# Seven buffers and a new order for the first adaLN weights, and the second condition's adaLN products on ScalarE and GpSimd, in a two-layer diffusion backbone step

## The chip, the cores and the metric

The kernel runs on one core of a Trainium2 chip. The time is in microseconds (us) of device time for one execution; less is better. The engines are called PE (TensorE, the matrix engine), DVE (VectorE), ACT (ScalarE), POOL (GpSimd) and SP (SyncE, which issues the transfers).

## The reference

One step of a hybrid backbone of two layers over 10 tiles of 128 tokens: eight tiles of latent tokens and two of context tokens, 1024 features each. What matters here is the start of a layer:

```python
def _rmsnorm(x, g):
    xf = x.astype(F32)
    y = xf * lax.rsqrt(jnp.mean(xf * xf, axis=-1, keepdims=True) + EPS)
    return (y * g.astype(F32)).astype(x.dtype)

def _adaln(cond, w, b):
    m = jax.nn.silu(cond) @ w + b
    shift, scale, gate = jnp.split(m[:, None, :], 3, axis=-1)
    return shift, scale, gate
```

Every layer does RMSNorm, multiplies by 1 + scale and adds shift, runs its mixer, multiplies by gate and adds the residual. There are two conditions: c for the latent tokens and c_ctx for the context tokens, so the product with the adaLN weights (1024 x 3072 for each layer) is needed for two vectors. Layer 0's mixer (here AB) starts with one projection (`w_in_ab`) that feeds windowed attention and an mLSTM memory with input and forget gates. Layer 1's (C) is latent attention. The output is the new tokens and the new caches and states.

## The kernel before, in words

The whole step is one program, written with helpers that record each operation. Apart from a middle part whose order is written by hand, a scheduler sets the order of the instructions on each engine; the program gives tiles, their buffers and the order in which work is asked for. A tile belongs to a tag with a number of buffers, and a new tile of the tag waits until the oldest one is no longer read.

*The start* (`layer_ab`, L718). A string of letters sets the order in which two sorts of work are asked for. For `x`, one token tile is loaded (`load_x`, L675, tag `xin`, 512 KB), normalised by its root mean square, and later transposed by PE (`xT_tile`, L522) and modulated (`xT_mod`, L533: on DVE, with a copy by ACT at L538 and a subtraction by DVE or POOL at L539 that splits the value into a high and a low half, `hTh` and `hTl`). For `m`, one of eight column groups of layer 0's shift and scale is made: `mod_load` (L239) loads two weight tiles of 128 columns each (tag `wm`, 512 KB each), `mod_start` (L252) multiplies them with both conditions on PE (`S<-wm,condT`), copies the result into a row (`mrow`, L262), and `columns` turns the row to columns by two small transposes (`S<-small,mrow`). The list `late` holds work back by two letters. At the letter of index 12 the weights of the first dense block are asked for (`blocks[0].load()`).

*The dense phase.* Then PE multiplies all tokens with `w_in_ab`, in blocks of 256 columns (the first has 272). Each block's weights are loaded (`wf`), ACT copies the high half (`wh`, L354) and POOL subtracts to get the low half (`wl`, L355). PE makes three products for each pair, high by high, high by low and low by high (L103 in the profile, the helper of all matmuls; transposes are at L107). The features come in eight parts, so a result takes 24 matmuls: 272 columns wide for each of ten token tiles in the first block, 512, 512 and 256 tokens wide in the others. A convolution (`cx`, L1465 on POOL, L1468 to L1475 on DVE) follows some blocks.

*The gates.* Woven into the dense phase is `gates` (L1294): it transposes the gate values (`GI`, `GF`), runs scans over tokens on DVE (L1371 to L1378), makes `LI` (L1401) and `rst` (L1410) and transposes both on PE again.

*The other adaLN columns* (`mod_steps`, L286) aren't made on PE: in each of eight steps a weight tile `mw` (128 x 512) is loaded, and DVE multiplies it by one number for each partition and adds it to `macc`, once for each condition (`cd` 0 and 1; L319 for the first step, L321 for the other seven). At the end PE sums `macc` over the partitions (`S<-macc,unit`) and DVE adds the bias (`bmod`, L306). Six blocks of 512 columns are made beside the dense phase, and blocks of 256 columns later, for layer 1's gate, in layer C.

Of the kernel before, what the change touches and what calls it, by code (L numbers as in the profile page):

```python
# [10 lines left out]
F32 = mybir.dt.float32  # L11
# [3 lines left out]
ALU = mybir.AluOpType  # L15
# [4 lines left out]
D = 1024  # L20
# [5 lines left out]
KD = D // 128  # L26
# [117 lines left out]
def body(tc, I, O, dbg=None, stop_at=None):  # L144
    K = Kern(tc, I, O, dbg)
    with ExitStack() as ctx:
        K.const = ctx.enter_context(tc.tile_pool(name="const", bufs=1))
        K.dram = ctx.enter_context(tc.tile_pool(name="dram", bufs=1, space=DRAM))
        K.left = lambda n: tc.alloc_tile_pool(name=n, bufs=1, side="left", reuse_waits="tile")
        K.right = lambda n: tc.alloc_tile_pool(name=n, bufs=1, side="right", reuse_waits="tile")  # L150
        K.set_psum(S=6, T=2)
        setup_consts(K)
        layer_ab(K)
        layer_c(K)
        K.set_psum()
# [84 lines left out]
def mod_load(K, pool, k):  # L240

    ws = []
    for i in range(2):
        w = K.t(pool, [128, KD, 128], F32, "wm", 4)
        f = slice(i * D + k * 128, i * D + (k + 1) * 128)
        K.dma(w, K.I["w_mod"][0, :, f].rearrange("(k p) f -> p k f", p=128))
        ws.append(w)
    return ws
# [37 lines left out]
def mod_steps(K, p, blocks, ahead, width=512):  # L286


    nc = K.nc
    parts = [(l, f, k) for l, f in blocks for k in range(KD)]  # L290
    asked = []

    def ask():
        if parts:
            l, f, k = parts.pop(0)
            w = K.t(p, [128, width], F32, "mw", ahead)
            K.dma(w, K.I["w_mod"][l, k * 128:(k + 1) * 128, f:f + width])
            asked.append(w)

    def total(l, f, acc):  # L300
        ps = K.ps()
        for cd in range(2):
            K.mm(ps[0:2, 0:width], K.sel[cd], acc[:, cd], cd == 0, cd == 1)
        bm = K.t(p, [2, width], F32, "bmod", 1)
        K.dma(bm, K.I["b_mod"][l:l + 1, f:f + width].to_broadcast([2, width]))
        nc.vector.scalar_tensor_tensor(bm, ps[0:2, 0:width], 0.5, bm, ALU.mult, ALU.add)  # L306
        K.dma(K.modd[l][:, f:f + width], bm)

    for _ in range(ahead):
        ask()  # L310
    late = None
    for l, f in blocks:
        acc = K.t(p, [128, 2, width], F32, "macc", 2)
        for k in range(KD):
            w = asked.pop(0)
            for cd in range(2):
                c = K.condT[:, cd * KD + k:cd * KD + k + 1]
                if k == 0:
                    nc.vector.tensor_scalar(acc[:, cd], w, c, None, ALU.mult)  # L319
                else:  # L320
                    nc.vector.scalar_tensor_tensor(acc[:, cd], w, c, acc[:, cd], ALU.mult, ALU.add)  # L321
            ask()
            if late and k == 5:
                late()
                late = None
            yield
        late = partial(total, l, f, acc)
    if late:
        late()
# [164 lines left out]
def rstd_of(K, pool, ss, n, eps, tag):  # L494
    nc = K.nc
    w = ss.shape[1]
    r = K.t(pool, [128, w], F32, tag, 4)
    nc.vector.tensor_scalar(r, ss, 1.0 / n, eps, ALU.mult, ALU.add)
    nc.gpsimd.tensor_tensor(r, r, K.mhalf.to_broadcast([128, w]), ALU.pow)
    return r  # L500
# [51 lines left out]
def x_src(K, tt):  # L552
    if tt < 8:
        return K.I["x_sample"][0, tt * 128:(tt + 1) * 128, :]
    return K.I["x_prompt"][0, (tt - 8) * 128:(tt - 7) * 128, :]
# [94 lines left out]
def layer_ab(K):  # L650
    nc, I = K.nc, K.I
# [20 lines left out]
    sp = left("start")  # L672
    setup_cond(K, sp)

    def load_x(tt):  # L675
        x = K.t(sp, [128, D], F32, "xin", 6)
        K.dma(x, x_src(K, tt))
        ss = K.t(sp, [128, 1], F32, "xss", 4)
        jk = K.t(sp, [128, D], BF16, "xjk", 1)
        nc.scalar.activation(jk, x, AF.Square, accum_out=ss)  # L680
        r = rstd_of(K, sp, ss, D, EPS, "xr")
        nc.vector.tensor_scalar(x, x, r[:, 0:1], None, ALU.mult)
        return x
# [4 lines left out]
    dense = Dense(blocks)  # L688
# [3 lines left out]
    def start_x(tt):  # L692
        x = load_x(tt)
        ci, i = chunk_of(tt)

        def rest():
            xT_tile(K, x, xT[ci][:, :, i * 128:(i + 1) * 128])
            if i == CHUNKS[ci][1] // 128 - 1:
                ready.append(ci)
                for j in done:  # L700
                    xT_mod(K, 0, ci, j, xT[ci][:, j, :])

        return rest

    def start_mod(k):
        ws = mod_load(K, sp, k)
        fin = mod_start(K, sp, k, ws)

        def rest():
            fin()  # L710
            done.append(k)
            for ci in ready:
                xT_mod(K, 0, ci, k, xT[ci][:, k, :])

        return rest

    xs, ks = iter(range(NT)), iter(range(KD))
    for n, a in enumerate("mxmxmxmxmxmxmxmxxx"):  # L718
        late.append(start_x(next(xs)) if a == "x" else start_mod(next(ks)))
        if n == 12:  # L720
            blocks[0].load()
        if len(late) > 2:
            late.pop(0)()
# [12 lines left out]
    zs[3].parts = 4  # L736
    mp = left("mod")
    dense.mods = mod_steps(K, mp, mods[0:2], 4)
    K.tp = gtp = left("gtmp")
    dense.run(1, 1)  # L740
# [4 lines left out]
    mp.release()  # L745
    mp = left("mod1")
    dense.mods = mod_steps(K, mp, mods[2:], 4)
    dense.run(3, 0.9)
    for _ in dense.mods:
        pass  # L750
    mod_cols(K, 1, mp)
# [5 lines left out]
    w = I["w_out_ab"][0]  # L757
# [40 lines left out]
    p = left("wo2")  # L798
# [11 lines left out]
    sp = right("cst")  # L810
# [1102 lines left out]
def layer_c(K):  # L1913
# [23 lines left out]
    nc.vector.tensor_scalar(ncol[:, 0:3], ps[:, 0:3], QSC, None, ALU.mult)  # L1937
    nc.vector.tensor_copy(ncol[:, 3:5], ps[:, 3:5])
    dense.mods = mod_steps(K, cm, [(1, 2 * D + f) for f in range(0, D, 256)], 4, 256)
    dense.run(3, 0.8)  # L1940
    for _ in dense.mods:
# [412 lines left out]
```

## Time and profile before

| What | Value |
|---|---|
| Three runs | 2618.43, 2617.19, 2615.36 us, median 2617.19 |
| Profiled execution | 2614.64 us, its span 2612.8 us |
| PE busy | 2563.6 us (98%) |
| DVE busy | 1779.5 us (68%) |
| ACT busy | 1411.7 us (54%) |
| POOL busy | 1161.8 us (44%) |

The span runs from the first to the last instruction of the profiled execution. A line of the table by stretch gives the busy time of each engine in a stretch of the span, with the number of instructions, PE's granted clock (1.00 is full speed), the share of the 16 DMA engines, and GB/s. A line of the waits names who waits, on which line, for whom, and us in total, times, and the longest. A line of groups gives the operation, its tiles (out<-in), shape and count, then busy us and mean ns of one, and the idle time before them. A line of the timeline gives the start, the duration, the operation, and in brackets the idle time before it and what ended it.

### The profile page before, as it was taken

What the parts mean: (1) busy time and instruction counts of PE and PEld (TensorE: products, weight loads), DVE (VectorE), ACT (ScalarE), POOL (GpSimd) and SP (SyncE); (2) the same over time, 40 slices, a digit from 0 to 9 for tenths busy, and PEclk for the clock granted to TensorE, in tenths of its full rate; (3) what the DMA queues carried; (4) which work ended last, traced back from release to release, by engine and by line L of the source; (5) the groups of instructions that cost most, each with busy time, mean ns of one, the idle gap of its engine ahead of it and who ended that gap; (6) DMA issues with size and microseconds to landing.
All of it is one profiled execution on the core that took longest, in us unless ns stands there. A gap on an engine that the chain in (4) does not pass through costs nothing. (4 is left out here: it accounts for less than half of the span.)

```text
span 2612.8 us, 48325 instructions
## 1 busy us (share of the span) xinstructions
PE 2563.6 (98%) x16233; PEld 2259.4 (86%) x16233; DVE 1779.5 (68%) x4045; ACT 1411.7 (54%) x3608; POOL 1161.8 (44%) x1549
## 2 busy tenths in 40 slices
PE   7999999999999999999999999999999999999998
PEld 6888898898898888887888878898899989999887
DVE  6994565656647676477777546526788888888754
ACT  5232444444434433477666433234788888888842
POOL 4342333423324344356445453224455545555832
PEclk9999999999999999999999999999999999999999
DMA  7565576566667664445443453523310101101333
GB/s 249 155 183 174 163 208 189 160 197 188 179 199 212 204 211 153 135 150 161 120 126 106 130 193 133 160 73 101 88 36 27 45 27 38 36 28 29 120 99 131
DMA packets 352970, 347.23 MB, mean 133 GB/s; under 512 B 36073, under 2 KB 297878, under 8 KB 352466
## 3 DMA queue, kind: packets, MB, share of 16 engines
q1 hardware_dynamic: 352722, 344.14, 43.2%
q8 instruction: 129, 2.11, 0.3%
q14 instruction: 119, 0.97, 0.1%
HBM read 233.52 MB, written 110.51 MB: 132 GB/s over the span
## 5 line engine op out<-in xcount | busy, mean ns | idle before, releaser
L355 POOL TENSOR_TENSOR wl<-wf,wh 128x256 fp32r<-128x256 f32 (+3 forms) x288 | 241.7, 864 | 435.8 <-ACT wh L354 381.2
L103 PE MATMUL mm<-hTh,wh 128*128 128x512 f32 (+1 forms) x912 | 329.0, 361 | 0.9 <-DVE scr L621 0.9
L103 PE MATMUL mm<-hTh,wl 128*128 128x512 f32 (+1 forms) x912 | 325.1, 356 | 0.0
L103 PE MATMUL mm<-hTl,wh 128*128 128x512 f32 (+1 forms) x912 | 325.0, 356 | 0.0
L103 PE MATMUL S<-cK,cQ 96*128 96x512 f32 (+3 forms) x1248 | 296.9, 364 | 2.2 <-ACT cPa L2256 1.3
L2304 DVE TENSOR_TENSOR cpl<-T,cph 128x512 fp32r<-128x512 f32 x336 | 228.6, 686 | 45.9 <-ACT cph L2303 42.8
L103 PEld LDWEIGHTS S<-cK,cQ 96*128 96x128 f32 (+1 forms) x1248 | 193.3, 189 | 25.4 <-ACT cPa L2256 3.5
L2303 ACT CAST cph<-T 128x512 fp32r<-128x512 f32 x336 | 192.4, 591 | 29.8 <-PE T L107 18.6
L103 PEld LDWEIGHTS mm<-hTh,wl 128*128 128x128 f32 x912 | 171.7, 188 | 26.6
L103 PEld LDWEIGHTS mm<-hTh,wh 128*128 128x128 f32 x912 | 171.6, 188 | 24.9 <-DVE scr L621 1.1
L103 PEld LDWEIGHTS mm<-hTl,wh 128*128 128x128 f32 x912 | 171.7, 188 | 23.2
L2254 DVE TENSOR_REDUCE cmx<-S 128x1 f32<-128x512 f32 x256 | 173.2, 682 | 16.7 <-PE S L103 15.2
L103 PE MATMUL V<-cph,cV 128*128 128x256 f32 x672 | 177.2, 290 | 1.1 <-DVE co L2319 0.8
L103 PE MATMUL V<-cpl,cV 128*128 128x256 f32 x672 | 172.1, 284 | 0.3 <-DVE cpl L2304 0.3
L1174 ACT CAST att_ph<-mm 128x512 fp32r<-128x512 f32 x168 | 98.6, 587 | 102.0 <-PE mm L107 100.7
L2235 POOL TENSOR_SCALAR cPa<-cPa,cst 128x512 f32<-128x512 f32 x128 | 98.7, 771 | 118.2 <-DVE cst L2232 97.6
L354 ACT CAST wh<-wf 128x256 fp32r<-128x256 f32 (+3 forms) x288 | 101.8, 409 | 74.9 <-DMA wf<-in_w_in_ab 42.8
L103 PE MATMUL mm<-wh,hTh 128*128 128x256 f32 x480 | 136.9, 285 | 4.0 <-DVE scr L1488 4.0
L1175 DVE TENSOR_TENSOR att_pl<-mm,att_ph 128x512 fp32r<-128x512 f32 x168 | 115.8, 689 | 34.8 <-ACT att_ph L1174 29.2
L1163 POOL TENSOR_SCALAR att_p<-att_p,att_den 128x640 f32<-128x640 f32 (+1 forms) x128 | 97.4, 774 | 86.9 <-DVE att_den L1160 39.1
L103 PE MATMUL mm<-wl,hTh 128*128 128x256 f32 x480 | 135.3, 282 | 0.1
L103 PE MATMUL mm<-wh,hTl 128*128 128x256 f32 x480 | 135.3, 282 | 0.0
(456 smaller groups left out, 7887.6 us busy)
## 6 DMA issues: line engine op xcount, KB each, us to landing
wf<-in_w_in_ab SPq DMA_DIRECT2D x120, 256.0 KB
in<-in SPq DMA_DIRECT2D x40, 514.0 KB
in<-in SPq DMA_DIRECT2D x32, 386.0 KB
mw<-in_w_mod SPq DMA_DIRECT2D x48, 256.0 KB
in<-scr SPq DMA_DIRECT2D x40, 258.0 KB
o_x<-y SPq DMA_DIRECT2D x20, 512.0 KB
wm<-in_w_mod SPq DMA_DIRECT2D x16, 512.0 KB
in<-cx SPq DMA_DIRECT2D x32, 256.0 KB
```

The costliest lines, as they stand in the source:

```text
L103: return self.nc.tensor.matmul(out, lhsT, rhs, start=start, stop=stop)
L354: K.nc.scalar.copy(wh, wf[:, k])
L355: K.nc.gpsimd.tensor_sub(wl, wf[:, k], wh.bitcast(F32))
L1163: nc.gpsimd.tensor_scalar(pv, pv, den[:, i:i + 1], 1.0, ALU.mult, ALU.mult)
L1174: K.nc.scalar.copy(ph, self.T)
L1175: K.nc.vector.tensor_sub(pl, self.T, ph.bitcast(F32))
L2235: nc.gpsimd.tensor_scalar(pv, pv, wt[:, c:c + 1], rd, ALU.mult, ALU.mult)
L2254: nc.vector.tensor_reduce(mx[:, b, c:c + 1], S, AX.X, ALU.max, negate=True)
L2303: nc.scalar.copy(ph, T_)
L2304: nc.vector.tensor_sub(pl, T_, ph.bitcast(F32))
```

## The change

The tag `wm` has seven buffers instead of four, `xin` four instead of six. The string of the start keeps eight `m` and ten `x` but has four pairs, then four `m`, then six `x`. In `mod_steps`, for blocks of 512 columns and the second condition (`cd` 1), the seven steps after the first are made by ACT, which multiplies the weight tile into a new tile `mq` (two buffers), and POOL, which adds it to `macc`: 42 operations of DVE become 42 of ACT and 42 of POOL. Lines from `mod_steps` on have numbers higher by four.

```diff
@@ mod_load
-        w = K.t(pool, [128, KD, 128], F32, "wm", 4)
+        w = K.t(pool, [128, KD, 128], F32, "wm", 7)
@@ mod_steps
                 if k == 0:
                     nc.vector.tensor_scalar(acc[:, cd], w, c, None, ALU.mult)
+                elif cd == 0 or width < 512:
+                    nc.vector.scalar_tensor_tensor(acc[:, cd], w, c, acc[:, cd], ALU.mult, ALU.add)
                 else:
-                    nc.vector.scalar_tensor_tensor(acc[:, cd], w, c, acc[:, cd], ALU.mult, ALU.add)
+                    q = K.t(p, [128, width], F32, "mq", 2)
+                    nc.scalar.mul(q, w, c)
+                    nc.gpsimd.tensor_add(acc[:, cd], acc[:, cd], q)
@@ layer_ab
-        x = K.t(sp, [128, D], F32, "xin", 6)
+        x = K.t(sp, [128, D], F32, "xin", 4)
...
-    for n, a in enumerate("mxmxmxmxmxmxmxmxxx"):
+    for n, a in enumerate("mxmxmxmxmmmmxxxxxx"):
```

SP's queue at the start, where the transfers of token tiles (`xin`), adaLN weights (`wm`) and the first dense weights (`wf`) are issued, before:

```order
L138 DMA xin_232<-in_x_sample 128x1024
L138 DMA xin_281<-in_x_sample 128x1024
L138 DMA xin_330<-in_x_sample 128x1024
L138 DMA xin_379<-in_x_sample 128x1024
L138 DMA xin_443<-in_x_sample 128x1024
L138 DMA wf_487<-in_w_in_ab 128x2x256
L138 DMA wf_487<-in_w_in_ab 128x2x16
L138 DMA wf_490<-in_w_in_ab 128x2x256
L138 DMA wm_253<-in_w_mod 128x8x128
L138 DMA wf_490<-in_w_in_ab 128x2x16
L138 DMA wm_255<-in_w_mod 128x8x128
L138 DMA wm_302<-in_w_mod 128x8x128
```

The same rows after the change:

```order
L138 DMA xin_232<-in_x_sample 128x1024
L138 DMA wm_253<-in_w_mod 128x8x128
L138 DMA wm_255<-in_w_mod 128x8x128
L138 DMA xin_281<-in_x_sample 128x1024
L138 DMA wm_302<-in_w_mod 128x8x128
L138 DMA xin_330<-in_x_sample 128x1024
L138 DMA wf_497<-in_w_in_ab 128x2x256
L138 DMA wf_497<-in_w_in_ab 128x2x16
L138 DMA wm_304<-in_w_mod 128x8x128
L138 DMA wf_500<-in_w_in_ab 128x2x256
L138 DMA wf_500<-in_w_in_ab 128x2x16
L138 DMA wm_351<-in_w_mod 128x8x128
```

The weight tiles wm_253 to wm_351 have moved ahead of the third and later token tiles, which are now issued between or behind them.

PE around the first matmul of the dense phase (`S_778<-wh`), before; `T` are transposes of token tiles, `S<-wm` products with adaLN weights:

```order
L107 MATMUL T_686<-small,xin_629 128x128 x4
L107 MATMUL T_692<-small,xin_629 128x128 x4
L103 MATMUL S_416<-wm_414,condT 2x128 x8
L107 MATMUL S_435<-small,mrow_372 128x2 x2
L103 MATMUL S_468<-wm_464,condT 2x128 x8
L103 MATMUL S_468<-wm_466,condT 2x128 x8
L107 MATMUL S_531<-small,mrow_433 128x2 x2
L103 MATMUL S_564<-wm_560,condT 2x128 x8
L103 MATMUL S_564<-wm_562,condT 2x128 x8
L107 MATMUL S_583<-small,mrow_485 128x2 x2
L107 MATMUL S_621<-small,mrow_581 128x2 x2
L103 MATMUL S_778<-wh_493,hTh_129 128x272
```

After the change:

```order
L103 MATMUL S_461<-wm_457,condT 2x128 x8
L107 MATMUL S_480<-small,mrow_400 128x2 x2
L107 MATMUL S_541<-small,mrow_447 128x2 x2
L107 MATMUL T_617<-small,xin_566 128x128 x4
L107 MATMUL T_623<-small,xin_566 128x128 x4
L103 MATMUL S_461<-wm_459,condT 2x128 x8
L107 MATMUL T_638<-small,xin_587 128x128 x4
L107 MATMUL T_644<-small,xin_587 128x128 x4
L107 MATMUL S_558<-small,mrow_478 128x2 x2
L103 MATMUL S_778<-wh_503,hTh_129 128x272
L103 MATMUL S_778<-wl_504,hTh_129 128x272
L103 MATMUL S_778<-wh_503,hTl_130 128x272
```

The transposes of the last two token tiles, which stood ahead of the dense phase, have moved into it, and one row of columns (mrow_478) stands right ahead of it where two stood.

POOL behind the start, before, where `wl` are the low halves of dense weights:

```order
L1368 MEMSET gB 36x1280
L1369 MEMSET gM 36x1280
L355 TENSOR_TENSOR wl_763<-wf_750,wh_762 128x256
L355 TENSOR_TENSOR wl_767<-wf_750,wh_766 128x256
L355 TENSOR_TENSOR wl_771<-wf_760,wh_770 128x256
L355 TENSOR_TENSOR wl_775<-wf_760,wh_774 128x256
L355 TENSOR_TENSOR wl_1203<-wf_1198,wh_1202 128x256
L355 TENSOR_TENSOR wl_1207<-wf_1198,wh_1206 128x256
L355 TENSOR_TENSOR wl_1213<-wf_1200,wh_1212 128x256
L355 TENSOR_TENSOR wl_1217<-wf_1200,wh_1216 128x256
```

After the change, with the additions to `macc` at L325:

```order
L1372 MEMSET gB 36x1280
L1373 MEMSET gM 36x1280
L325 TENSOR_TENSOR macc_906<-macc_906,mq_942 128x512
L325 TENSOR_TENSOR macc_906<-macc_906,mq_978 128x512
L325 TENSOR_TENSOR macc_906<-macc_906,mq_1014 128x512
L325 TENSOR_TENSOR macc_906<-macc_906,mq_1050 128x512
L325 TENSOR_TENSOR macc_906<-macc_906,mq_1095 128x512
L359 TENSOR_TENSOR wl_763<-wf_750,wh_762 128x256
L325 TENSOR_TENSOR macc_906<-macc_906,mq_1140 128x512
L359 TENSOR_TENSOR wl_767<-wf_750,wh_766 128x256
L359 TENSOR_TENSOR wl_771<-wf_760,wh_770 128x256
L359 TENSOR_TENSOR wl_775<-wf_760,wh_774 128x256
```

Six additions of the second condition now stand in this queue ahead of and between the low halves, which keep their order.

DVE at the gates, between the first scan (`gM`) and the next ones (`gB`), before; `cx` is the convolution:

```order
L1468 SCALAR_TENSOR_TENSOR cx_1567<-scr_1524,cw,cx_1567 128x512
L306 SCALAR_TENSOR_TENSOR bmod_1532<-S_1529,bmod_1532 2x512
L1378 SCALAR_TENSOR_TENSOR gM<-LF,m_1363,LI 4x1024 x2
L1371 SCALAR_TENSOR_TENSOR gB<-rst,LF 4x1280
L1372 SCALAR_TENSOR_TENSOR gB<-rst,LF 4x1280
L1378 SCALAR_TENSOR_TENSOR gM<-LF,LI 4x256 x2
```

After the change:

```order
L1479 SCALAR_TENSOR_TENSOR cx_1593<-scr_1597,cx_1593 128x512
L1382 SCALAR_TENSOR_TENSOR gM<-LF,m_1381,LI 4x1024 x2
L1456 MEMSET scr_1639 128x1
L1462 MEMSET scr_1639 128x1
L1479 SCALAR_TENSOR_TENSOR cx_1602<-scr_1606,cx_1602 128x512
L306 SCALAR_TENSOR_TENSOR bmod_1654<-S_1651,bmod_1654 2x512
L1472 SCALAR_TENSOR_TENSOR cx_1643<-scr_1639,cw,cx_1643 128x256
L1375 SCALAR_TENSOR_TENSOR gB<-rst,LF 4x1280
L1376 SCALAR_TENSOR_TENSOR gB<-rst,LF 4x1280
L1382 SCALAR_TENSOR_TENSOR gM<-LF,LI 4x256 x2
```

The scans keep their order, but two convolution steps and the bias (`bmod`) now stand between the first scan and the next ones, where nothing stood.

More of the change, by code (lines that the diff above doesn't have):

```diff
@@ L747, in layer_ab @@
     dense.mods = mod_steps(K, mp, mods[2:], 4)
-    dense.run(3, 0.9)
+    dense.run(3,0.9)
     for _ in dense.mods:
```

## The prediction

> **What bounds the kernel now.** I read the page first (its line of busy times), then the busy time by stretch of the program, then the waits of TensorE (PE).
>
> ```profile
> PE 2563.6 (98%) x16233; PEld 2259.4 (86%) x16233; DVE 1779.5 (68%) x4045; ACT 1411.7 (54%) x3608; POOL 1161.8 (44%) x1549
> ```
>
> TensorE is busy for 2563.6 of 2612.8 us, so everything that can be won without removing matmuls lies in 49 us of idle time and in time at a low clock. The table by stretch says where. Its columns are length, busy PE, weight loads, VectorE (DVE), ScalarE (ACT), GpSimd (POOL), granted clock, DMA share, GB/s.
>
> ```profile
> 6.60:16.00 9.40, 9.37 (x65) 6.31 (x65) 1.20 (x5) 2.97 (x6) 0.73 (x2) 1.00 1.08 375
> 16.00:57.60 41.60, 34.52 (x287) 25.50 (x286) 35.15 (x66) 28.68 (x63) 25.74 (x29) 1.00 0.88 278
> 57.60:66.00 8.40, 8.38 (x55) 8.37 (x56) 7.60 (x20) 2.90 (x6) 5.77 (x6) 0.80 0.04 5
> 66.00:130.00 64.00, 64.00 (x388) 54.10 (x386) 58.39 (x120) 15.69 (x40) 22.87 (x21) 1.00 0.52 157
> 130.00:149.00 19.00, 14.96 (x89) 12.63 (x89) 17.81 (x34) 8.88 (x15) 11.99 (x8) 0.91 0.35 88
> 180.00:230.00 50.00, 50.00 (x374) 44.50 (x374) 33.67 (x60) 9.57 (x27) 11.50 (x12) 1.00 0.63 194
> 230.00:1074.00 844.00, 839.00 (x5424) 758.46 (x5423) 506.67 (x1306) 351.97 (x933) 320.15 (x398) 1.00 0.62 188
> ```
>
> Three things are to be seen. The start (16 to 57.6) leaves PE idle for 7.1 us. The stretch where the gates are computed (130 to 149) leaves 4.0. From 230 on PE is full, 839 of 844 us: what is won before that point is carried to the end, and nothing in the part behind can pay back or eat much. Note DVE in 66 to 130: 58.39 of 64, yet PE is full there, so a lighter DVE wins nothing in that stretch. The waits of PE behind the start, in us (total, times, longest), name what is left:
>
> ```profile
> PE S L107 <- ACT mrow L262: 3.2, 1, 3.2
> PE T L107 <- ACT rst L1410: 2.2, 1, 2.2
> PE T L107 <- DVE LI L1401: 1.6, 1, 1.6
> PE S L103 <- DVE bmod L306: 1.4, 1, 1.4
> ```
>
> These 8.4 us and the idle time of the start are all that the change can reach before 230.
>
> **Change, part 1: order of the start, seven weight buffers, four token buffers.** The dense phase begins when all eight adaLN columns are there. Work of PE up to that point, and the rate of the loads (the same table columns as above), and the last steps:
>
> ```profile
> L103 PE MATMUL S<-wm,condT 128*2 128x128 f32 x193 | 22.5, 273 | 0.0
> L107 PE MATMUL T<-small,xin 128*128 128x128 f32 x80 | 11.6, 282 | 3.7 <-DVE xT L528 2.7 <-ACT xT L530 0.9
> L107 PE MATMUL S<-small,mrow 2*128 2x2 f32 x14 | 2.0, 207 | 0.2 <-ACT mrow L262 0.2
> ...
> 0.00:6.00 6.00, 0.04 (x1) 0.04 (x1) 0.85 (x6) 1.59 (x2) 0.19 (x4) 1.00 0.56 162
> 6.00:42.00 36.00, 32.17 (x248) 23.26 (x249) 22.28 (x49) 23.30 (x48) 16.05 (x20) 1.00 1.07 351
> 42.00:48.00 6.00, 6.00 (x55) 4.45 (x53) 5.25 (x8) 2.94 (x8) 4.95 (x6) 1.00 0.91 278
> ```
>
> ```profile
> 46.33 0.37 SPq L138 DMA_DIRECT2D wm<-in_w_mod  x1
> 57.62 0.28 PE L107 MATMUL S<-small,mrow 2*128 2x2 f32 x2 [3.25 <-ACT mrow L262]
> 57.83 0.39 PE L103 MATMUL S<-wh,hTh 128*128 128x272 f32 x1
> ```
>
> Now all ten tokens go through before the dense phase, and the last weight tile is issued only at 46.33. In the new order tokens 8 and 9 are transposed inside the dense block.
> - By PE: 22.5 + 11.6 + 2.0 = 36.1 us of work stand between 16.0 and the dense start; two of ten tokens less are 16/80 x 11.6 = 2.3 us less. 16.0 + 33.8 gives 49.8 as the earliest start.
> - By DMA: up to the last weight tile the new order loads 16 x 0.524 MB of weights, 8 x 0.524 of tokens, 4 x 0.278 of dense weights and 0.4 of small ones, 14.1 MB. The rows move 0.97 MB by 6 us and 12.6 more by 42, at 278 GB/s the rest: all is there at 44. Behind it come the last products, the row, its columns and the modulation; from 46.33 plus a load to 57.83 these took at most 11.5 us now, so 44 lands between 50 and 53.
>
> I take 50.3: 7.5 us earlier than 57.83. The 2.3 us of transposes are not saved, they move behind the start: **A = -5.2 us** (ends: start at 47.5 gives -8, at 53.5 gives -2.0). Freed token buffers are not missed: at four, a token's load waits for the one four earlier, and the tokens now come late. On SP each load that waits for its buffer holds all behind it; the weights, which had four buffers, no longer wait.
>
> The clock:
>
> ```profile
> 60.00:61.00 1.00, 1.00 (x6) 1.00 (x6) 1.00 (x5) 0.73 (x2) 0.49 (x1) 0.50 0.00 0
> 62.00:63.00 1.00, 1.00 (x8) 1.00 (x8) 1.00 (x3) 0.59 (x2) 0.09 (x1) 0.73 0.00 0
> 146.00:148.00 2.00, 2.00 (x7) 1.61 (x7) 2.00 (x4) 0.09 (x1) 0.00 (x0) 0.53 0.07 15
> ```
>
> Shortly after the pause of 3.25 us at 57.62 the granted clock was 0.50; by the stretch 57.6 to 66 (0.80 over 8.4 us) that costs 8.4 x 0.20 = 1.7 us. It came again after the 2.2 us pause at 142.76 (0.91 over 19 us: 1.7 us). With no long wait for the last row ahead of the dense start the first one goes: **B = -1.7** (0 if a wait stays). The Trainium skill ("TensorE: Matmul & The Clock Gate", Part 1: The HAM clock gate) has a throttle that closes after a free-running window of some 3.4 us without work. The trace agrees on the length of the slow time but shows it after a pause of 2.2 us too. By the page alone B would be the same.
>
> **Part 2: the gates.** The order moves the gate work against the matmuls, so the two waits there are recomputed.
>
> ```profile
> 113.07 1.05 PE L107 MATMUL T<-small,GF 128*36 128x128 f32 x8
> ...
> 119.86 0.28 PE L103 MATMUL S<-hTl,wh 128*128 128x256 f32 x1
> 119.98 0.28 PE L103 MATMUL S<-hTh,wl 128*128 128x256 f32 x1
> ...
> 124.80 0.40 PE L103 MATMUL S<-hTl,wh 128*128 128x512 f32 x1
> 125.03 0.40 PE L103 MATMUL S<-hTh,wl 128*128 128x512 f32 x1
> ...
> 134.19 0.78 PE L107 MATMUL T<-small,LI 36*128 36x36 f32 x10 [1.61 <-DVE LI L1401]
> ```
>
> ```profile
> 132.03 2.02 DVE L1401 TENSOR_TENSOR LI<-LI,gB 36x1280 f32<-36x1280 f32 x1
> 130.68 0.71 ACT L354 CAST wh<-wf 128x256 fp32r<-128x256 f32 x2 [8.88 <-DMA wf<-in_w_in_ab]
> ```
>
> From GF's transposes to LI the chain on DVE takes 134.05 - 113.07 = 21.0 us, and PE covers 134.19 - 113.07 - 1.61 = 19.5 of it. A wide matmul costs 0.23 us (125.03 - 124.80), a half one 0.12. In the new order 48 wide and 29 half ones stand there instead of 56 and 24: 1.2 us less cover, 18.3. DVE's own order puts two convolution steps and a bias (0.5 to 0.8 us each) between the scans and takes one out behind them, some 1.3 us more, so the chain becomes 22.3 and the wait 4.0. Between LI and rst nine wide ones come to four half ones less, 1.6 us more cover, and DVE has about as much less to do there, so the 2.2 us wait goes to 0. **C = 4.0 + 0 - 1.6 - 2.2 = +0.2**; the low clock stays, since a pause of 4.0 is left. Ends: all 3.8 go and the clock with them, -5.5; or the last GF copy is late. That copy stands on ACT behind two casts that now wait for dense weights (8.88 us in the row of ACT): +4.
>
> **Part 3: 42 products from DVE to ACT and POOL.** Prices, of DVE's product, POOL's subtraction of dense weights, POOL's subtraction of the tokens, which has the new addition's shape, ACT's cast of that shape, and POOL's convolution:
>
> ```profile
> L321 DVE SCALAR_TENSOR_TENSOR macc<-mw,condT,macc 128x512 f32<-128x512 f32 x84 | 67.1, 839 | 7.3 <-DMA mw<-in_w_mod 7.2
> L355 POOL TENSOR_TENSOR wl<-wf,wh 128x256 fp32r<-128x256 f32 x40 | 44.3, 1134 | 68.4 <-ACT wh L354 57.3 <-PE S L103 11.1
> L539 POOL TENSOR_TENSOR hTl<-xT,hTh 128x512 fp32r<-128x512 f32 x8 | 11.9, 1491 | 9.0 <-ACT hTh L538 9.0
> L538 ACT CAST hTh<-xT 128x512 fp32r<-128x512 f32 x16 | 9.4, 618 | 11.6 <-DVE xT L537 11.6
> L1465 POOL TENSOR_SCALAR cx<-scr,cw 128x512 f32<-128x512 f32 x8 | 9.1, 1135 | 22.0 <-ACT scr L1450 12.3 <-PE S L103 7.6 <-DVE scr L1458 2.1
> ```
>
> ```profile
> 206.65 4.34 POOL L355 TENSOR_TENSOR wl<-wf,wh 128x256 fp32r<-128x256 f32 x4 [11.06 <-PE S L103]
> ```
>
> DVE loses 42 x 0.839 = 35.2 us, POOL gains 42 x 1.49 = 62.6, ACT 42 x 0.62 = 26.0 (priced by the cast), and all of this lies beside a full PE. What comes to the path is the order on POOL: it works its queue in order, so the weight halves (wl), for which PE waits, stand behind additions that wait for loads. Five dense blocks fill 66 to 235, 34 us each; each needs 8 x 1.13 + 3 x 1.1 = 12.4 us of POOL, and eight additions 11.9: 24.3 of 34. There is room. With less DVE work the 1.4 us wait for bmod goes: **D = -1.4** (0). Two new waits are likely. In the dense start the tiles' results are emptied from PSUM by DVE, which then still modulates tokens 8 and 9, so that a bank comes free about one or two of its 0.84 us instructions late, 1 us. And the second condition's sum, which now passes two engines, reaches its selecting matmul about one addition later, 1 us after what PE has to do meanwhile: **E = +2.0** (0 to +8). Layer C is scheduled anew as well; PE is full there: **F = 0** (-3 to +3).
>
> The Trainium skill ("SBUF — State Buffer", SBUF: two separate sides) speaks against this part: a DVE operation with two inputs in SBUF and a GpSimd one hold a shared port against each other, one waits for the whole other. In the trace four wl took 4.34 us while DVE ran products, 1.09 each, so they were hindered and not shut out. By the rule 42 additions of 1.49 would shut DVE out for 62.6 us to save it 35.2.
>
> Sum: -5.2 - 1.7 + 0.2 - 1.4 + 2.0 = **-6.1**. The profiled execution took 2614.64 us (span 2612.8 and 1.8 around it), 2.55 below the median of the runs. 2608.5 for a profiled one, 2611.1 against the median of 2617.19; I say 2611.
>
> **Rivals.**
> - *Better*: both waits at the gates and their low clock go (C = -5.5). For it: the wait of 1.6 is short, and DVE is lighter by 14 products ahead of GF. Against: the order leaves less cover. -5.2 - 1.7 - 5.5 - 1.4 + 2.0 = -11.8: 2605.4.
> - *The loads set the start*: the rate (1.07 of the DMA engines up to 42 us) is the limit, the dense phase begins at 53.5, and a wait for the last row stays. A = -2.0, B = 0: -1.2, 2616.0. That is the change not doing what it says.
> - *The gates eat it*: the last GF copy waits on ACT for dense weights; C = +4.2: -2.1, 2615.1.
> - *Slower: POOL falls behind.* Additions contended by DVE's products. From 2.7 us for one ((34 - 12.4) / 8) POOL is over its 34 us per block and PE waits for wl; with wl at the price of a contended one it is earlier. At 3.2 us each it is 4 us over per block, 5 blocks, +20: -6.1 + 20 = +13.9, 2631. For it: POOL's prices vary with DVE's work. Against: 1.49 is a price measured beside a busy DVE (7.60 of 8.40 us).
>
> **How the numbers follow.** A measurement of this kernel can tell about 0.2% from no change, 5.2 us: faster is below 2612.0, slower above 2622.4. Forecast 0.45, better 0.17, loads 0.13, gates 0.13, POOL 0.10, nothing at all 0.02. The forecast lies just inside faster, so I count 0.27 of it as faster and 0.18 as same; with the better case and 0.06 of the two middle ones faster is 0.50, same 0.40, slower 0.10. The range leaves out POOL's case and the outer part of the better one: 2603 to 2620.
>
> **What would show it.** Right: the first 272 wide matmul near 50 us, clock 1.00 behind it, a wait of about 4 us for LI, none for rst and bmod, PE's busy time from 230 on unchanged. Wrong: the dense start after 53, PE waiting for wl or for macc for more than 3 us in all, additions of over 2.5 us, or a different idle time of PE behind 1000 us.

## The result, and the profile after

The changed kernel took 2631.5 us (median of 4 runs, 2630.5 to 2633.35) against 2617.69 for the kernel before (4 runs): a ratio of 1.0053, 95% interval 1.004 to 1.0065. It is 13.8 us slower. The forecast was 2611, with a range of 2603 to 2620. Two executions among the experiments below took far longer at a low clock (4199.82 us with the new start and a light DVE, 3125.91 with the products alone and memsets), and all medians below leave them out.

The dense phase began as early as forecast, but most of what follows it did not come as forecast. Here is the table by stretch of the changed kernel, with the columns of before:

```profile
16.00:57.60 41.60, 38.98 (x330) 30.91 (x329) 30.25 (x56) 26.11 (x55) 21.72 (x25) 1.00 0.87 283
57.60:66.00 8.40, 5.51 (x42) 5.07 (x40) 8.40 (x11) 2.77 (x5) 5.96 (x5) 1.00 0.00 1
66.00:130.00 64.00, 60.37 (x348) 49.88 (x349) 60.53 (x123) 29.73 (x68) 49.82 (x41) 0.97 0.55 167
130.00:149.00 19.00, 12.91 (x68) 11.22 (x67) 18.61 (x29) 3.62 (x7) 10.28 (x6) 0.84 0.22 54
149.00:180.00 31.00, 29.41 (x192) 25.04 (x191) 27.04 (x41) 13.28 (x26) 17.74 (x16) 0.99 0.51 140
180.00:230.00 50.00, 41.85 (x295) 38.01 (x295) 40.95 (x49) 20.50 (x44) 38.55 (x30) 0.90 0.69 213
```

Up to 57.6 TensorE (PE) is busier by 4.5 us. Behind that it is idle in every stretch, 8.2 us of it in 180 to 230, where it had no idle time before, and its granted clock fell to 0.90. POOL went from 22.87 to 49.82 us in 66 to 130, and DVE did not become lighter there: 60.53 instead of 58.39. The waits of PE in the first 300 us:

```profile
PE T L107 <- DVE scr L1456: 6.1, 1, 6.1
PE S L107 <- DVE crow L217: 6.0, 1, 6.0
PE T L107 <- DVE xin L686: 4.8, 2, 2.8
PE S L103 <- ACT wh L358: 3.9, 1, 3.9
PE T L107 <- DVE GI L1334: 3.3, 1, 3.3
PE S L103 <- POOL wl L359: 2.9, 4, 1.6
PE S L103 <- POOL macc L325: 2.4, 1, 2.4
```

The 6.0 for `crow` was there before too. The first line is the wait for LI (its tile is named in the row of 144.97 below; DVE ran a small instruction at that moment). The timeline of PE at the places that count, the changed kernel:

```profile
49.98 0.39 PE L103 MATMUL S<-wh,hTh 128*128 128x272 f32 x1
...
60.70 0.40 PE L103 MATMUL S<-wh,hTh 128*128 128x272 f32 x1 [0.38 <-ACT hTh L542]
...
66.32 1.06 PE L107 MATMUL T<-small,xin 128*128 128x128 f32 x8 [2.83 <-DVE xin L686]
...
144.97 1.25 PE L107 MATMUL T<-small,LI 36*128 36x36 f32 x10 [6.09 <-DVE scr L1456]
...
208.06 0.79 PE L103 MATMUL S<-wh,hTh 128*128 128x256 f32 x2 [3.91 <-ACT wh L358]
...
245.21 0.50 PE L103 MATMUL mm<-hTh,wh 128*128 128x512 f32 x1
```

The last row is the first matmul of the hand-ordered part, which stood here before:

```profile
227.41 0.50 PE L103 MATMUL mm<-hTh,wh 128*128 128x512 f32 x1
```

It comes 17.8 us later, and the rows add up to that. The dense start is 7.85 us earlier. Two tokens' transposes inside it take 2.1, waits there 0.4 + 2.8. The waits for GI (3.3) and LI (6.1 for 1.6) add 7.8, those for wl, wh and macc 9.3 (2.7 more for wl, 3.9 for wh, 2.4 + 0.3 for macc); rst and bmod give back 3.6. That is +11.0. The low clock cost 3.4 us before (two times 1.7) and costs 1.9 + 3.0 + 0.3 + 5.0 = 10.2 now (lost share times length, from 66 on in the table): +6.8. Together 17.8. PE's last matmul came 15.9 us later, so 1.9 us came back behind 245 us. What gave them back is not shown: the same matmuls were 17.4 us late at 1087 us of the kernel before, 16.3 at 1509 and 18.1 at 1844.

### The profile page after: what moved, and what is told of

The parts are those of the page before. It is cut to its first block, busy times and chain, and to the rows that moved or that the text cites. A ratio compares the mean times of both kernels' runs of the same rounds, so it can differ in the third digit from the quotient of the medians.

```text
span 2628.7 us, 48416 instructions
## 1 busy us (share of the span) xinstructions
PE 2569.5 (98%) x16233; PEld 2263.6 (86%) x16233; DVE 1786.9 (68%) x4003; ACT 1439.5 (55%) x3650; POOL 1223.1 (47%) x1591
## 4 chain that ended last, share of the span: by engine, by line
PE 82%; DVE 3%; issue 3%; DMA 2%; ACT 2%; POOL 2%; SPq 1%; POOLq 0%; DVEq 0%; ACTq 0%
PE mm L103 33%; PE S L103 27%; PE V L103 9%; PE T L107 6%; PE D L103 3%; PE mm L107 3%; SPq L138 1%; DMA mw<-in_w_mod 1%; PE T L103 1%; POOL wl L359 1%; DMA o_x<-y 0%; DMA w<-in_w_out_ab 0%; DVE cx L1472 0%; POOL w L913 0%; DMA att_q<-ql 0%
## 5 line engine op out<-in xcount | busy, mean ns | idle before, releaser
L103 PEld LDWEIGHTS mm<-hTl,wh 128*128 128x128 f32 x912 | 171.7, 188 | 23.2
L1179 DVE TENSOR_TENSOR att_pl<-mm,att_ph 128x512 fp32r<-128x512 f32 x168 | 115.7, 689 | 35.2 <-ACT att_ph L1178 29.7
L103 PEld LDWEIGHTS V<-cph,cV 128*128 128x128 f32 x672 | 126.5, 188 | 8.3 <-DVE co L2323 1.4
```

The lines of the kernel that those rows point to most:

```text
L103: return self.nc.tensor.matmul(out, lhsT, rhs, start=start, stop=stop)
L1179: K.nc.vector.tensor_sub(pl, self.T, ph.bitcast(F32))
```

## The experiments

Each kernel was timed beside the kernel before. P is the theory that the products on ScalarE (ACT) and GpSimd (POOL) cost; P1 puts it down to POOL's queue, P2 to additions and DVE's products that hinder each other. O is the theory that the new start costs: O1 by the order of its letters, O2 because any earlier start is handed back. T and V ask why it is handed back: T because the last tokens and the gates come late, V because DVE is full whatever the start does.

| Run | us (median) | before, beside it | ratio, 95% interval |
|---|---|---|---|
| order and buffers alone | 2622.63 | 2618.14 | 1.0011 to 1.0029 |
| products alone | 2637.82 | 2618.14 | 1.0064 to 1.0090 |
| memsets for the additions | 2621.65 | 2618.14 | 1.0006 to 1.0025 |
| additions left out | 2617.79 | 2618.14 | 0.9993 to 1.0011 |
| buffers alone | 2620.32 | 2618.68 | 0.9997 to 1.0014 |
| order alone, sum later | 2618.48 | 2618.68 | 0.9987 to 1.0005 |
| changed kernel, sum later | 2630.31 | 2618.68 | 1.0031 to 1.0056 |
| string in between | 2621.92 | 2618.68 | 1.0005 to 1.0023 |
| five and six buffers | 2617.69 | 2618.85 | 0.9987 to 1.0004 |
| six and five buffers | 2622.58 | 2618.85 | 1.0002 to 1.0019 |
| new start, light DVE | 2612.77 | 2618.85 | 0.9970 to 0.9988 |
| old start, light DVE | 2618.24 | 2618.85 | 0.9990 to 1.0008 |
| copies for the additions | 2620.41 | 2618.84 | 0.9998 to 1.0015 |
| additions on DVE | 2622.62 | 2618.84 | 1.0004 to 1.0021 |
| products alone, memsets | 2625.61 | 2618.84 | 1.0014 to 1.0038 |

### The two halves apart

The first run has the changed buffers and string, and `mod_steps` of before; the second has the new `mod_steps` and the start of before.

> The new order and buffers of the start alone, all products on VectorE as before. In the changed kernel the dense phase begins 7.9 us earlier (57.83 to 49.98), gives 2.1 back for two tokens' transposes and 3.2 in waits for token 9, and the low clock of 1.7 goes. Theory P (the products on ScalarE and GpSimd are what costs): this alone is faster than before, by 3 to 7 us, 2611 to 2615, and TensorE waits for GI and LI together no more than 4 us. Theory O (the order of the start pushes the gates out of their cover): most of the loss is here, slower than before by 5 to 12 us, with the waits for GI (3.3) and LI (6.1) as in the changed kernel.

> The 42 products on ScalarE and GpSimd alone, start as before. Theory P: slower than before by 15 to 22 us (2633 to 2640), since the start's gain is missing too; waits for wl, wh and macc of 8 us or more between 150 and 230 us as in the changed kernel. Theory O: within 6 us of before.

Neither theory alone holds. The products alone cost 19.7 us, which is P's, but the order alone costs 4.5 too, where P had it faster and O had 5 to 12 and a wait for GI, which did not come. Its waits, in the stretch up to 260 us, and the stretch that lost most:

```profile
PE S L103 <- DVE macc L321: 10.5, 1, 10.5
PE T L107 <- DVE xin L682: 4.8, 2, 2.9
PE T L107 <- DVE LI L1401: 4.2, 1, 4.2
```

```profile
149.00:180.00 31.00, 20.52 (x132) 17.27 (x132) 26.28 (x55) 10.22 (x23) 11.62 (x12) 0.78 0.64 193
```

With all products on DVE, the time won at the start comes back as a wait for the sum of the third block of columns, and with it a low clock: 0.22 x 31 = 6.8 us. In the kernel with the products alone the longest wait is for the high half of dense weights, 11.5 us, on ACT.

### Is it POOL's queue, or the hindrance?

The additions of the changed kernel are replaced by memsets (`mq` is then 1120 wide), or left out. In both kernels the second condition's sums lack what the additions would bring.

```diff
-                    nc.gpsimd.tensor_add(acc[:, cd], acc[:, cd], q)
+                    nc.gpsimd.memset(q, 0.0)
+                    nc.gpsimd.memset(q[:, 0:256], 0.0)
```

> The changed kernel with each addition of GpSimd replaced by two memsets of about the same time together that read nothing; the second condition's sums are left out beyond their first term. Theory P1 (GpSimd's queue: the low halves of the dense weights stand behind the additions): as slow as the changed kernel within 5 us, with the waits for wl, while VectorE's product comes back to about 0.84 us. Theory P2 (additions and VectorE's products hinder each other, 1.29 us for a product where it was 0.84): VectorE's product back to 0.84 to 0.9 us and the time near the new order alone, 2611 to 2618.

> The changed kernel without GpSimd's additions, ScalarE's products kept; the second condition's sums are left out beyond their first term. Theories P1 and P2 alike: near the new order alone or 1 to 4 us better, since VectorE is lighter by 35 us: 2608 to 2615. If ScalarE's products cost (weight tiles held for longer, casts of dense weights behind them): slower than the new order alone by 3 us or more.

With memsets the time is 2621.65, 9.9 us less than the changed kernel. That lies between the two ranges, above P2's 2611 to 2618; without additions it is 2617.79, above the 2608 to 2615 that both theories had. POOL's own price of a pair of memsets, 1.36 us, is close to that of an addition, 1.53. Groups of the changed kernel (up to 240 us), then of the kernel with memsets and the one without additions (up to 260 us):

```profile
L325 POOL TENSOR_TENSOR macc<-macc,mq 128x512 f32<-128x512 f32 x42 | 64.2, 1529 | 15.1 <-ACT mq L324 12.5 <-DVE scr L1493 0.9 <-DVE macc L319 0.5
L321 DVE SCALAR_TENSOR_TENSOR macc<-mw,condT,macc 128x512 f32<-128x512 f32 x42 | 54.0, 1286 | 8.6 <-DMA mw<-in_w_mod 8.0
```

```profile
L325 POOL MEMSET mq<- 128x1120 f32 x42 | 42.9, 1041 | 19.5 <-ACT mq L324 19.5
L326 POOL MEMSET mq<- 128x256 f32 x42 | 12.7, 318 | 0.1
L321 DVE SCALAR_TENSOR_TENSOR macc<-mw,condT,macc 128x512 f32<-128x512 f32 x42 | 34.8, 830 | 24.9 <-DMA mw<-in_w_mod 24.5
```

```profile
L321 DVE SCALAR_TENSOR_TENSOR macc<-mw,condT,macc 128x512 f32<-128x512 f32 x42 | 35.2, 839 | 17.2 <-DMA mw<-in_w_mod 16.7
```

A product of DVE took 0.839 us before, 1.286 beside the additions, 0.830 beside memsets, 0.839 without them. The product's time is on P2's side: POOL being busy with memsets did not lengthen it, and the additions did.

The kernel without additions is still 3.9 us faster than the one with memsets. That is not the price of POOL's queue alone, because the memsets hinder DVE in another place: in its operations with one tensor as input. The first step of each sum (L319), with memsets and then without additions, and a wait of PE in the kernel with memsets:

```profile
L319 DVE TENSOR_SCALAR macc<-mw,condT 128x512 f32<-128x512 f32 x12 | 12.1, 1046 | 5.1 <-DMA mw<-in_w_mod 5.1
```

```profile
L319 DVE TENSOR_SCALAR macc<-mw,condT 128x512 f32<-128x512 f32 x12 | 6.7, 601 | 3.0 <-DMA mw<-in_w_mod 3.0
```

```profile
109.44 1.89 PE L107 MATMUL T<-small,GI 128*36 128x128 f32 x8 [3.80 <-DVE scr L1459]
```

Ahead of that wait two copies of GI on DVE took 2.64 us together, where without additions they took 0.26; they ended at 109.39, just behind two memsets of POOL, at 109.35. How the 3.9 us divide between the queue and this is not shown.

The memsets had taken away one thing more, the sums' dependence on POOL. Three more runs test that: a copy in the addition's place (dependence kept, one input read; only the last term of the sum is left), the additions on DVE (everything is computed), and the memsets with the old start.

```diff
-                    nc.gpsimd.tensor_add(acc[:, cd], acc[:, cd], q)
+                    nc.gpsimd.tensor_copy(acc[:, cd], q)
...
+                    nc.vector.tensor_add(acc[:, cd], acc[:, cd], q)
```

> The changed kernel with each of GpSimd's additions replaced by a copy of ScalarE's product into the sum (one input instead of two; TensorE and ScalarE still wait for it as for the addition; the second condition's sums keep only the last term). Theory P2 (additions and VectorE's products hinder each other): a copy reads half as much and is shorter, so VectorE's product lies between 0.83 (memsets) and 1.29 us, and the time between 2622 and 2628. Rival D (the sums' dependence on GpSimd, which the memsets had taken away too, is what the 10 us were): 2629 to 2632 with the waits for wl, wh and macc of the changed kernel, whatever the product's time.

> The changed kernel with the 42 additions on VectorE instead of GpSimd; everything is computed. VectorE then has as many operations of two inputs as in the new order alone, and ScalarE's products are extra. Theory P2: VectorE's product is back near 0.84, an addition takes 0.7 to 1.1, and the time is that of the new order alone within 4 us, 2619 to 2627. Rival (ScalarE's products and the weight tiles that they hold for longer cost by themselves): 2628 or more.

> The products alone, with the old start, and memsets in place of the additions (the second condition's sums keep their first term). The products alone took 2637.8, 19.7 more than before. Theory P2: most of that goes, 2617 to 2625, with VectorE's product at 0.8 to 0.85 us. Rival P1 (GpSimd's queue and the wait for wh of 11.5 us at 184 us come from its order): 2630 or more.

The copy gives 2620.41, so the dependence alone is not what cost; it was even better than P2's range of 2622 to 2628. (A dependence on operations as long as the additions was not run by itself; what shows of it are PE's waits for macc in the changed kernel, 2.7 us.) Groups of that kernel, then of the one with additions on DVE:

```profile
L321 DVE SCALAR_TENSOR_TENSOR macc<-mw,condT,macc 128x512 f32<-128x512 f32 x42 | 37.3, 887 | 27.9 <-DMA mw<-in_w_mod 27.3
L325 POOL COPY macc<-mq 128x512 f32<-128x512 f32 x42 | 29.9, 713 | 24.9 <-ACT mq L324 19.3 <-DVE macc L321 4.8 <-POOL macc L325 0.2
```

```profile
L321 DVE SCALAR_TENSOR_TENSOR macc<-mw,condT,macc 128x512 f32<-128x512 f32 x42 | 34.1, 815 | 3.6 <-DMA mw<-in_w_mod 3.5
L325 DVE TENSOR_TENSOR macc<-macc,mq 128x512 f32<-128x512 f32 x42 | 32.0, 764 | 0.3 <-ACT mq L324 0.2
```

An addition takes 0.764 us on DVE and 1.529 on POOL, and on DVE the product stays at 0.815. That kernel took 2622.62, the time of the order alone: beside a DVE as full as there, ACT's products cost nothing on top. Beside a light DVE they do, as the table at the end of the next part shows. The copy occupies POOL for 29.9 us and the addition for 64.2, so the copy does not separate reading from occupation; the memsets, with 55.6 us, do. With the old start the memsets brought the products from 2637.82 to 2625.61: 12 of their 19.7 us, just over P2's range of 2617 to 2625. Another 6.8 us are left there, which the same table takes up.

### Where the gain of the start went

First the pieces of the start: buffers alone with the old string, a string in between, and the sum asked for later (`k == 7` for `k == 5`) in the order alone and in the changed kernel.

> Seven and four buffers alone, the old string and VectorE's products. Theory O1 (the string's run of four m ahead of the last tokens makes token 9 late and moves the gates): with the old string the wait for token 9 (2.9 us) goes and the time is before's or up to 6 us better. Theory O2 (any earlier dense start is handed back, since VectorE's products and scans, not TensorE, set the sums and gates behind it): the dense phase begins earlier, by 4 to 7 us, and the time is within 3 us of the new order alone, 2620 to 2625, with waits for macc or LI of over 8 us together.

> Seven and four buffers, VectorE's products, and a string between the old and the new one (six pairs, two m, four x). Theory O1: the fewer m stand ahead of the last tokens, the less is handed back: 2612 to 2618, no wait for token 9. Theory O2: like the new order alone, 2620 to 2625.

> The new order and buffers, VectorE's products, and each block's sum (the selecting matmul over macc) asked for two steps later, at step 7 of the next block instead of 5. In the new order alone TensorE waited 10.5 us for macc at 178 us and ran at 0.78 of its clock in that stretch. Theory O2a (the place of the sum in TensorE's order is what hands the start's gain back): the wait falls under 4 us and the time to 2608 to 2615. Rival (VectorE itself is behind, the wait appears at the next thing that it feeds): 2619 to 2625.

> The changed kernel with each sum asked for two steps later. Theory P2 (what costs is that additions and products hinder each other): VectorE's product stays at about 1.29 us and the time falls by no more than 5 us, 2626 to 2632. Rival (the sum waits for GpSimd's late additions, and its place is what costs): 2615 to 2622.

The dense phase of the buffers alone begins at 49.97: the buffers bring the early start, and the string adds nothing to it. The gain goes the same way (1.6 us slower than before, within the noise; with the whole new string it was 4.5, so the string may cost something itself). Waits of PE with the buffers alone:

```profile
PE S L103 <- DVE macc L321: 9.3, 1, 9.3
PE T L107 <- DVE xin L682: 4.1, 3, 3.0
PE T L107 <- DVE LI L1401: 2.5, 1, 2.5
```

The string in between shows the same three waits, 9.3, 3.9 and 2.9 us. O2 holds, O1 falls. With the sum later the wait falls to 5.8 us and the time to that of before, not under it, so its place is a part of the matter; the 2618.48 lie between O2a's range, which ended at 2615, and the rival's, which began at 2619. In the changed kernel the later sum moves 1.2 us only, with products at 1.23 us, as P2 had it.

Next, the number of buffers, and DVE's load. Five and six, then six and five buffers, with the old string; then both starts with the second condition's 42 products left out and nothing in their place.

> Five buffers for the weights, six for the tokens as before, the old string, VectorE's products: tokens 8 and 9 stay ahead of the dense phase. Theory T (with seven and four buffers the last tokens move behind the dense start, so the gates come late and VectorE's chain ends later): here the dense phase begins 2 to 6 us earlier than before with no wait for token 9 and GF not later than in before, and the gain stays: 2612 to 2617. Rival V (VectorE is full up to 180 us whatever the start does): 2617 to 2621, a longer wait for LI, rst or macc taking the place of the gain.

> Six and five buffers, the old string, VectorE's products: token 9 alone moves behind the dense start. Theory T: between the kernel with five and six and the one with seven and four (2620), with a wait for token 9 of 2 to 3 us and a wait for macc at about 176 us of 3 to 8. Rival V: the same time as five and six within 2 us.

> The new order and buffers, with the second condition's 42 products left out and nothing in their place (its sums keep their first term): VectorE is lighter by about 34 us, nothing is added to ScalarE or GpSimd. Theory V (VectorE's load hands the start's gain back): the wait for macc (10.5 us in the new order alone) is gone, and against the next kernel, which has the old start, this is 4 us or more faster. Theory T: the macc wait is gone, but the wait for LI stays (4 to 7 us), and it is within 3 us of the next kernel.

> The kernel before with the same 42 products left out. What a lighter VectorE is worth by itself with the old start: by the waits of before that VectorE ends (LI 1.6, bmod 1.4, and rst behind them 2.2 with a low clock of 1.7) 2 to 6 us, 2612 to 2617. Theory V expects it slower than the kernel with the new order and the same products left out by 4 us or more, theory T within 3.

With five and six the dense phase begins at 56.49, only 1.3 us earlier, and LI (3.0), bmod (2.3) and the last row (3.2) are still waited for. Its 2617.69 lie in V's range and just above T's, but the start that T asked for, 2 to 6 us earlier, did not come, so this is hardly a test of T. Six and five took 2622.58, no better than seven and four, where T had it between and V had the time of five and six within 2 us: both missed. The dense phase of its profiled execution began at 58.62, later than before, and PE waited 5.1 us for wl, so this run decides nothing either. The waits of the kernel with the new start and a light DVE:

```profile
PE T L107 <- DVE scr L1452: 6.1, 1, 6.1
PE T L107 <- DVE xin L682: 3.8, 2, 1.9
```

The wait for macc is gone, and this is the only run clear of before on the fast side: 5.5 us faster than the old start with the same light DVE, where with a full one the new start is 4.5 us slower. What a lighter DVE is worth with the old start is 0.6 us, within the noise: the waits of before, read as its price, had promised 2 to 6. V holds, with the part of T that LI is still waited for, 6.1 us: that chain is DVE's scans themselves and does not shrink with the products (23.2 us from GF's transposes to LI's in the order alone, 24.0 here).

Side by side, the runs form steps (medians, us):

| The second condition's 42 products | old start | new start |
|---|---|---|
| on DVE | 2618.1 to 2618.9 | 2622.63 |
| left out | 2618.24 | 2612.77 |
| ACT multiplies, nothing is added | not run | 2617.79 |
| ACT multiplies, POOL runs memsets | 2625.61 | 2621.65 |
| ACT multiplies, POOL adds | 2637.82 | 2631.50 |

With the new start a lighter DVE wins 9.9 us. ACT's products take back 5.0, the memsets 3.9 more, and additions in place of memsets 9.9 more. With the old start a lighter DVE wins 0.6, ACT's products and the memsets together cost 7.4, and the additions 12.2 more: the 6.8 us left above are the price of ACT's products and the memsets there. Not all of these kernels were timed beside each other, and the median of the kernel before moved by 1.2 us between timings, so a step is good to 1 to 2 us.

The 5.0 us of ACT's products stand where its queue holds up the casts of dense weights. Four of these casts ran at 189.83 us where the products are left out, and at 196.50, behind products that waited for their loads, where they are kept. From 180 to 230 us PE was busy for all of the 50 us at a clock of 1.00 without them, and for 47.1 us at 0.93 with them.

## Why the prediction was wrong, point by point

**The start** came at 49.98, where 50.3 was forecast and 49.8 was the earliest by PE's work. That it fits so closely is partly luck: the 33.8 us of work were added up from busy times that overlap, and PE worked for 31.4 us between 16.0 and 49.98 and stood idle for 2.6. In the other kernels with seven and four buffers it came between 49.5 and 51.8. The wait for the last row and its low clock went (B, -1.7: clock 1.00 in 57.6 to 66).

**A (-5.2) was mis-sized, by one queue.** Measured are -7.85 + 2.1 + 3.2 = -2.5. The prediction let tokens 8 and 9 move behind the start for the price of their transposes on PE. The timeline of DVE in the changed kernel shows their other half:

```profile
51.46 8.91 DVE L541 TENSOR_SCALAR xT<-xT,A,B 128x512 f32<-128x512 f32 x9
...
62.17 3.35 DVE L543 TENSOR_TENSOR hTl<-xT,hTh 128x512 fp32r<-128x512 f32 x2
65.44 0.74 DVE L686 TENSOR_SCALAR xin<-xin,xr 128x1024 f32<-128x1024 f32 x1
```

Token 9's normalisation (L686) stands in DVE's queue behind nine modulations and their splits, and PE's transposes wait for it. E had allowed 1 us for what this queue holds up; it was 3.2.

**The failed step is in part 3: "DVE loses 42 x 0.839 = 35.2 us ... and all of this lies beside a full PE".** DVE's products took 67.1 us before and 54.0 after: it lost 13.1. Each of the 42 that stayed became 0.45 us longer, since POOL's additions run beside them. Other operations of DVE grew too, L319 from 0.63 to 0.94 us each. Over the whole execution DVE was busy for 1779.5 us before, for 1754.3 without the additions and for 1786.9 in the changed kernel: what the move freed, 25.2 us, the additions took back with 32.6, so DVE did not become lighter at all. The price of the addition was right (1.49 forecast, 1.53 measured). In DVE's timeline one sees single products of 1.67, 1.10 and 1.66 us:

```profile
95.01 1.67 DVE L321 SCALAR_TENSOR_TENSOR macc<-mw,condT,macc 128x512 f32<-128x512 f32 x1
...
97.43 1.10 DVE L321 SCALAR_TENSOR_TENSOR macc<-mw,condT,macc 128x512 f32<-128x512 f32 x1
...
98.56 1.66 DVE L321 SCALAR_TENSOR_TENSOR macc<-mw,condT,macc 128x512 f32<-128x512 f32 x1
```

The Trainium skill ("SBUF — State Buffer", SBUF: two separate sides) has an operation of DVE with two inputs in SBUF and a GpSimd operation that reads SBUF exclude each other: the later one waits for the whole of the other. The runs bear it out: memsets, which read nothing, left the product at 0.830. The prediction set the rule beside four wl that were "hindered and not shut out" and took none of it into the sum. Four at 1.09 us each were that hindrance (the shortest wl of that kernel took 0.72), and it had to be priced on the other engine too.

**C (+0.2) was +5.6.** The wait for rst went, as forecast. LI was waited for 6.1 us, not 4.0, and GI, which the prediction didn't look at, 3.3. From GF's transposes to the end of LI the chain took 23.7 us instead of the 22.3 of the sum, and PE covered 17.8 of it instead of 18.3. Without additions GI isn't waited for and LI is still 6.9, so the wait for GI comes from what POOL does (with memsets it was 3.8), and the wait for LI does not need the additions. In the order alone, with a full DVE, LI was waited for 4.2 us, close to the forecast.

**E (+2.0) was +9.3**, and the low clock behind those pauses came on top. The prediction's sign of being wrong, more than 3 us of waits for wl or macc, came with 2.9 + 2.7 = 5.6 us. High halves are cast on ACT. In ACT's timeline the casts stand behind products that wait for POOL's additions to free `mq`, and for their loads:

```profile
204.11 0.72 ACT L324 ACTIVATE mq<-mw,condT 128x512 f32<-128x512 f32 x1 [2.17 <-POOL macc L325]
...
206.07 1.37 ACT L324 ACTIVATE mq<-mw,condT 128x512 f32<-128x512 f32 x2 [0.98 <-DMA mw<-in_w_mod]
207.35 0.35 ACT L1491 CAST scr<-S 128x256 fp32r<-128x256 f32 x1
207.60 0.41 ACT L358 CAST wh<-wf 128x256 fp32r<-128x256 f32 x1
```

PE's 3.91 us wait ends with that cast. The prediction named what is queued behind the additions on POOL, and not what is queued behind the products on ACT.

**D (-1.4)** was right. **F** was set at 0 within -3 to +3; what came back behind 245 us is 1.9, inside these bounds.

**The slower rival** named 2631 and 2631.5 came, but by another way: additions of 2.7 us and more, POOL over its 34 us for a block. They took 1.53, and the memsets, nearly as long on POOL, cost 3.9 of the additions' 13.7. So the number isn't to its credit, though waits for wl (2.9 us) were part of it.

**"A lighter DVE wins nothing in that stretch"** read 58.39 of 64 us from PE's side only. DVE had little slack from 57.6 to 180: it was busy for 7.60 of 8.40 us, 58.39 of 64, 17.81 of 19, and 29.81 of 31 in the last stretch, here in the kernel before:

```profile
149.00:180.00 31.00, 29.64 (x199) 26.00 (x198) 29.81 (x53) 8.13 (x22) 12.86 (x12) 1.00 0.70 198
```

An earlier PE then only waits at the next thing that DVE feeds: 10.5 us at macc in the order alone. With the old start a lighter DVE did win nothing that is clear of noise (0.6 us), but with the new one it won 9.9.

What stays open is how the 3.9 us of the memsets divide between POOL's queue and DVE's hindered operations, and what the dependence on long additions adds by itself. Three kernels have a clock of 0.90 between 16 and 50 us in their profiled execution (products alone; old start, light DVE; six and five buffers), and their dense phase began at 58.6 to 60.6 instead of 57.83. The executions of the kernel before alone spread from 2612 to 2624 us, so a part of single differences of 1 to 3 us may come from such a low clock at the start.

## What to carry to other kernels

Before work is moved from a full engine to an idle one, look at what both do at the same moment: the gain is the moved work less what the remaining work gets slower by, and here DVE won 25.2 us of busy time and lost 32.6. When PE's start comes earlier, ask which engine must feed it next and how full that one is in the stretch behind; a start that the feeder can't follow is handed back as a pause, and most pauses of 2.2 us and more cost a low clock on top here. An instruction added to a queue is priced by what stands behind it there when it waits.

## What the runs showed of the hardware

Additions of POOL and products of DVE, each with two inputs, slowed the product from 0.84 to 1.29 us; memsets of nearly the same total time did not (0.83), and copies, of half the time, hardly (0.89). Memsets did slow operations of DVE with one tensor input: L319 took 1.05 us beside them and 0.60 without additions. The same addition took 0.76 us on DVE and 1.53 on POOL, there beside DVE's products (the shortest 1.26).

The clock dropped to about a half after most pauses of PE of 2.2 us and more, not after all. The changed kernel's 6.1 us pause for LI was followed by 0.50 to 0.54 up to 150 us, and the two pauses at 208 and 210 by a longer time:

```profile
209.00:211.00 2.00, 0.40 (x2) 0.34 (x2) 2.00 (x3) 2.00 (x6) 2.00 (x3) 0.50 0.03 12
211.00:213.00 2.00, 1.87 (x8) 1.58 (x8) 1.97 (x3) 0.06 (x1) 2.00 (x2) 0.50 0.87 240
...
217.00:219.00 2.00, 2.00 (x15) 2.00 (x15) 1.60 (x3) 0.00 (x0) 1.32 (x1) 0.72 0.90 301
```

But the pauses of 2.83 us that ended at 66.32 and of 2.44 us that ended at 184.79 were followed by a clock of 1.00, up to 72 and 190 us. A pause's length alone doesn't tell.
